# Cross attention: memory keys projected among the output projection, queries in a row, memory values behind them, head norms taken from raw projections

## The chip, the cores and the metric

The kernel runs on one core of a Trainium2 chip. What is measured is the device time of one execution in microseconds (us). Before the change it is 1073.2 us, the median of three runs (1072.76 to 1074.09).

The engines are named as in the profile: PE is TensorE's matmul side and PEld its weight loads, DVE is VectorE, ACT is ScalarE, POOL is GpSimd, and SP issues the DMAs. Each engine works through its own queue in the order in which the program put its instructions there, and waits on semaphores for the others.

## The reference, cut to what matters

One layer: three token mixers and a gated sum of them, an output projection with a residual, cross attention into a memory of 256 tokens, and a gated MLP. x has 512 tokens of 1024 channels. The change lies in the stretch from the output projection to the first matmuls of the MLP.

```python
def rmsnorm(x, g):
    xf = x.astype(jnp.float32)
    y = xf * lax.rsqrt(jnp.mean(xf * xf, axis=-1, keepdims=True) + EPS)
    return (y * g.astype(jnp.float32)).astype(x.dtype)

def memory_cross_attention(h, m, w_q, w_kv, q_g, k_g, w_o):
    q = rmsnorm(heads(h @ w_q, MEM_HEADS), q_g)          # 4 heads of 128
    k, v = jnp.split(m @ w_kv, 2, axis=-1)
    k = rmsnorm(heads(k, MEM_HEADS), k_g)
    v = heads(v, MEM_HEADS)
    s = jnp.einsum("bqhd,bkhd->bhqk", q, k).astype(jnp.float32) * MEM_DIM ** -0.5
    p = jax.nn.softmax(s, axis=-1).astype(v.dtype)
    o = jnp.einsum("bhqk,bkhd->bqhd", p, v).reshape(B, S, MEM_W)
    return o @ w_o

x = x + mixed @ w_out[l]
x = x + memory_cross_attention(rmsnorm(x, norm_xq[l]), rmsnorm(mem, norm_mem[l]), ...)
x = x + conv_ffn(rmsnorm(x, norm_ffn[l]), ...)
```

A norm over a row multiplies it by one number. The query of a head is the projection of a normed row, normed again over the head's 128 channels, so the first norm's factor cancels out of the second except in its epsilon.

## The kernel before

**Layout.** Channels lie on the 128 partitions and tokens along the free axis, so a projection of 1024 channels to 128 is eight blocks of 128x128 weights against tiles of 512 tokens (256 for the memory). A unit is 128x1024 weights, 512 KB, loaded into `wraw` (three buffers). Every matmul of a projection is done in float32r with both operands split into a high and a low part: `split_unit` makes `whi` on ACT (line 154) and `wlo` on DVE (line 155), two buffers each; activations are split by `split` and `split_scaled`. `mm3` then issues, for each block, whi times the high part (line 175) and whi times the low part (line 176), and at the end wlo times the high parts (line 178): 24 matmuls for each unit.

**The stages around the change.** `wo0` to `wo7` are the eight tiles of the output projection. After each, `residual` adds x on DVE (line 770), squares on ACT (line 772), and splits the result for the next projection (`xqh` on ACT, line 167; `xql` on DVE, line 168). The memory is loaded at this point too (`mem_sb`), split into `memh`/`meml` and squared. The norms' sums over channels are matmuls with a matrix of ones in plain float32: `memps` (line 783), `xqps` (line 799), `xfps` (line 871), and, inside each head, `mkn0p` to `mkn3p` and `mqn0p` to `mqn3p` (line 229, the `light` form of `head_norm`). `rsqrt` makes the factor with Ln, Exp and Square on ACT (lines 216 to 218) and two instructions on DVE (219, 220).

**The heads.** The string `CROSS` gives the order in which the steps are written: k is a key head (`memory_key`: projection `mk`, times `r_mem` on DVE, head norm), q a query head (`memory_query`: projection `mq`, times `r_xq` on DVE, head norm), w the weights of a head (`memory_weights`), v the values (`memory_values`: `mv`, four units of weights for two tiles of 128 tokens). `memory_weights` treats a head in two halves g: scores `msc` in float32 (line 829), row maxima on DVE (830), Exp on ACT (833, each followed by a read of the accumulated sum), reciprocal and scaling on DVE (834, 836), four transposes `mT` on PE (840) and a copy `mpt` on ACT (842). Then `mo` (line 860) multiplies with the values, `ym` splits the result, and `wmo0` to `wmo7` project back. `up` is the MLP's first projection; its outputs are multiplied with `r_f`, the factor from `xfps`, on DVE (line 885).

**What sets the order.** The code's order is not the order of the queues: a scheduler moves instructions on each engine after its own estimate of when they can run. PSUM is shared out in pools: three banks for projections (`d`), three for sums and scores (`m`), two for the transposes (`g`); a tile waits for the reader of the one whose bank it takes. In the row names a trailing number is a head or a unit, then a half: `msc21` is head 2, second half; `whi97` is the high part of unit 97, the first of `wmo`.

Of the kernel before, what the change touches and what calls it, by code (L numbers as in the profile page):

```python
# [9 lines left out]
F32 = mybir.dt.float32  # L10
# [12 lines left out]
CROSS = "k0 q0 k1 q1 w0 k2 q2 w1 k3 q3 w2 w3 v"  # L23
# [43 lines left out]
def build(nc, tc, ctx, x_t, mem_t, w, cols_d, const_d, unit_d, out_t, dbg=None):  # L67
# [14 lines left out]
    work = tiles_of("work", "n", 4)        # short-lived  # L82
# [30 lines left out]
    def in_one_go(after, tiles, func):  # L113
        """func on tiles in place, behind the instruction `after`, with one load of its table"""
        with tc.issue_after(after.ins), tc.high_priority():
            for t in tiles:
                S.activation(t, t, func)
            exp_ln_tables()
# [11 lines left out]
    eps = col("eps")  # L130
    gains = cols[:, COLS["fox_q"]:COLS["onorm"] + 1]
# [5 lines left out]
    units = {}  # L137

# [9 lines left out]
    def split_unit(u):  # L148
        """a unit of the weight stream as an exact sum of two float32r operands"""
        raw = units.pop(u) if u in units else load_unit(u)  # L150
        hi = wp.tile([P, 1024], F32R, tag="whi", name=f"whi{u}", bufs=WB[1])
        lo = wp.tile([P, 1024], F32R, tag="wlo", name=f"wlo{u}", bufs=WB[2])
        for s in [slice(0, T), slice(T, 2 * T)] if u == 0 else [slice(0, 2 * T)]:
            S.activation(hi[:, s], raw[:, s], AF.Copy)  # L154
            V.tensor_tensor(lo[:, s], raw[:, s], hi[:, s].bitcast(F32), ALU.subtract)  # L155
        return hi, lo

    def split(src, alloc, name):
        """src as hi + lo"""
        hi = alloc(name + "h", F32R)  # L160
        lo = alloc(name + "l", F32R)
        S.activation(hi, src, AF.Copy)
        V.tensor_tensor(lo, src, hi.bitcast(F32), ALU.subtract)
        return hi, lo
# [6 lines left out]
    def mm3(ps, unit, blocks, xs, first, last):  # L171
        """ps += the blocks of a unit times xs, without the product of the low parts"""
        hi, lo = unit
        for i, (b, (xh, xl)) in enumerate(zip(blocks, xs)):
            PE.matmul(ps, hi[:, b], xh, start=first and i == 0, stop=False)  # L175
            PE.matmul(ps, hi[:, b], xl, start=False, stop=False)  # L176
        for i, (b, (xh, _)) in enumerate(zip(blocks, xs)):
            PE.matmul(ps, lo[:, b], xh, start=False, stop=last and i == len(xs) - 1)  # L178
# [24 lines left out]
    def project_heads(u, ys, name, n=4):  # L203
        """[512, 1024] weights, two output tiles in a unit"""
        for g in range(n):
            unit = split_unit(u + g)
            for q in range(2):
                ps = dense_ps(f"{name}{2 * g + q}")
                mm3(ps, unit, [block(4 * q + k) for k in range(4)], ys, True, True)
                yield 2 * g + q, ps  # L210

    def rsqrt(ps, name, scale, n=T, work=work):
        """-2 / sqrt(ps * scale + eps), with a Newton step"""
        a = work(name + "a", F32, n)
        b = work(name + "b", F32, n)
        S.activation(a, ps, AF.Ln, bias=eps, scale=scale)
        S.activation(a, a, AF.Exp, scale=-0.5)
        S.activation(b, a, AF.Square, scale=math.sqrt(scale))
        V.scalar_tensor_tensor(b, ps, EPS / scale, b, ALU.add, ALU.mult)
        V.scalar_tensor_tensor(a, b, -3.0, a, ALU.add, ALU.mult)  # L220
        return a

    def head_norm(src, name, scale, n=T, work=work, psum=misc_ps, light=False):
        """-2 / sqrt(sum of src^2 * scale + eps) on every partition"""
        sq = work(name + "s", F32, n)
        S.activation(sq, src, AF.Square)
        ps = psum(name + "p")
        if light:
            PE.matmul(ps[:, :n], ones, sq, start=True, stop=True)
        else:  # L230
            hi, lo = split(sq, lambda name, dt: work(name, dt, n), name)
            PE.matmul(ps[:, :n], ones_r, hi, start=True, stop=False)
            PE.matmul(ps[:, :n], ones_r, lo, start=False, stop=True)
        return rsqrt(ps[:, :n], name, scale, n, work)
# [107 lines left out]
    def convolve(g, base):  # L342
        """silu(conv(projection)) of the tiles of q, k or v"""
        conv[g] = cs = [ptile(f"{g}{h}") for h in range(H)]
        for h in range(H):
            t, c, w = raws[g][h], conv[g][h], 4 * (base + h)
            last = S.activation(c, t, AF.Copy, scale=col("gdn_conv", w + 3))
            for i in (1, 2, 3):
                V.scalar_tensor_tensor(c[:, i:], t[:, :T - i], col("gdn_conv", w + 3 - i), c[:, i:], ALU.mult, ALU.add)
        in_one_go(last, cs, AF.Silu)  # L350

# [9 lines left out]
    def scalars():  # L361
# [25 lines left out]
        # token on partition: [.., token block, row]  # L387
# [5 lines left out]
        # beta, beta * exp(gc), exp(g_last - gc)  # L393
# [4 lines left out]
    def select(ps, kind, h, stop=True):  # L398
        """a row of the scalars on every partition"""
# [20 lines left out]
    def prep_head(h):  # L420
# [6 lines left out]
        # the decay, [j, i] by chunks, 0 for j > i  # L427
# [13 lines left out]
        # A^T without its factors beta_i, and attn^T  # L441
# [15 lines left out]
        # token-major keys and values  # L457
# [13 lines left out]
    # the inverses of the 32 x 32 diagonal blocks of I + A by elimination, a block's  # L471
    # even or odd columns on a partition
# [30 lines left out]
    def expand(dst, src, h):  # L503
        """the 32 x 32 blocks of a head on the diagonals of its chunks"""
# [13 lines left out]
    def invert(h):  # L518
        """(I + A)^-T of the chunks from that of the blocks on their diagonals: with D these and
        M = A D^-1 without these blocks, M^4 = 0 and (I + A)^-1 = D^-1 (I - M + M^2 - M^3)"""  # L520
# [47 lines left out]
    def qkv_head(u, h, name, norm, alloc):  # L568
        """q^T, k^T and [key, dv] by key blocks"""
# [20 lines left out]
    def packed(name, kinds):  # L590
        """[P, 128], .. [P, 512] of each kind, the halves of a kind's tile shared"""
# [191 lines left out]
    PE.matmul(ps[:, :M], ones, acc, start=True, stop=True)  # L783
    for t in range(2):
        PE.matmul(ps[:, M + t:M + t + 1], acc[:, t * P:t * P + P], ones[:, 0:1], start=True, stop=True)
    r_mem = ztile("r_mem")
    V.tensor_scalar(r_mem[:, :M + 2], rsqrt(ps[:, :M + 2], "rmem", 1.0 / D, M + 2), -0.5, None, ALU.mult)

# [1 line left out]
    acc = None  # L790
    xq = []
    for m in range(KC):
# [3 lines left out]
        xq.append(s)  # L796
    x2 = xr
    ps = misc_ps("xqps")
    PE.matmul(ps, ones, acc, start=True, stop=True)
    r_xq = cp.tile([P, T], F32, tag="rh", name="r_xq")  # L800
    V.tensor_scalar(r_xq, rsqrt(ps, "rxq", 1.0 / D), -0.5, None, ALU.mult)

# [1 line left out]
    def memory_key(h):  # L804
        ps = project(UNITS["mk"] + h, xs_mem, f"mk{h}", M)
        if h % 2 == 0:
            mem_k.append(ztile(f"memk{h}"))
        kn = mem_k[h // 2][:, h % 2 * M:h % 2 * M + M]
        V.tensor_tensor(kn, ps[:, :M], r_mem[:, :M], ALU.mult)
        r = head_norm(kn, f"mkn{h}", 1.0 / P, M, work=nwork, light=True)  # L810
        V.scalar_tensor_tensor(kn, kn, col("mk"), r, ALU.mult, ALU.mult)

    def memory_query(h):
        ps = project(UNITS["mq"] + h, xq, f"mq{h}")
        q = ztile(f"mqT{h}")
        V.tensor_tensor(q, ps, r_xq, ALU.mult)
        r = head_norm(q, f"mqn{h}", 1.0 / P, work=nwork, light=True)
# [28 lines left out]
    def memory_values():  # L846
        for t, ps in enumerate(project_tokens(UNITS["mv"], xs_mem, "mv", 2)):
            v = vwork(f"memv{t}")
            S.activation(v, ps, AF.Copy, scale=r_mem[:, M + t:M + t + 1])
            mem_v.append(v)  # L850

    mem_k, mem_v, qs, pts = [], [], [], []
    for step in CROSS.split():
        {"k": memory_key, "q": memory_query, "w": memory_weights, "v": lambda h: memory_values()}[step[0]](int(step[1:] or 0))
# [16 lines left out]
    PE.matmul(ps, ones, acc, start=True, stop=True)  # L871
# [55 lines left out]
def unit_columns():  # L927
    """[P, 32, 16]: the even (on even partitions) or odd columns of the unit matrix"""
# [4 lines left out]
def layout(inputs):  # L933
# [3 lines left out]
    def tiles(a, n):  # L937
        """[K, M] -> [units, P, 1024] streaming (output tile, k chunk) blocks of [P, 128]"""
# [88 lines left out]
```

## Time and profile before

| | |
|---|---|
| median of three runs | 1073.2 us |
| profiled execution: span from first to last instruction | 1072.4 us |
| PE busy | 1055.4 us, 98% of the span |
| DVE, ACT busy | 638.3 us, 556.3 us |
| output projection, wo0 to wo7 | 556.62 to 602.11 |
| keys, queries, values, weights of head 0 and scores of head 1 | 602.11 to 656.07 |
| from the last value matmul to the first wmo matmul | 656.07 to 676.18 |
| wmo0 to wmo7 | 676.18 to 699.54 |
| MLP | 699.54 to the end |

Times in a stage are from the start of the span. A row of the timeline gives the start, the length, the engine, the line, the operation and the tiles (out<-in); "x8" are eight instructions in a row, and then the length goes to the end of the last. PE starts a matmul before the one before it has ended, so what a matmul costs is the distance between starts, not its length. "[2.47 <-DVE mp L836]" is idle time of the engine ahead of the row, and what ended it. In a table of stretches each engine has its busy time and, in brackets, the count of instructions; PEclk is the granted TensorE clock as a share of 2.4 GHz.

### The profile page before, as it was taken

To read this page: it belongs to the slowest core of one execution; us is meant where nothing else is said; L and a number is where in the kernel's file an instruction comes from. 1 tells how busy PE (TensorE), PEld (TensorE's weight loads), DVE (VectorE), ACT (ScalarE), POOL (GpSimd) and SP (SyncE) were. 2 spreads that over 40 slices of the span, in tenths; PEclk is the share of its full clock that TensorE was granted. 3 is DMA by queue.
4 is the path that set the end of the run, shared out by engine and by line. 5 is a ranking of instruction groups with operands and counts; after the bars stand their busy time and mean duration, and the time that the engine had idled before them with its cause. 6 is when DMAs were issued, how large, how long until landed. Compare 5 with 4: busy or idle time off the path is not lost.

```text
span 1072.4 us, 12705 instructions
## 1 busy us (share of the span) xinstructions
PE 1055.4 (98%) x4868; PEld 858.3 (80%) x4868; DVE 638.3 (60%) x1002; ACT 556.3 (52%) x894; POOL 31.6 (3%) x81
## 2 busy tenths in 40 slices
PE   6999999999999999999999998999999999999998
PEld 4887888778888888888888886778888888888886
DVE  5987566886454443454577667667776667742221
ACT  6689677856263646574546557544444444431110
POOL 0000100101010000000000000000000000000000
PEclk9999999999999999999999999999999999999999
DMA  5232212121211122122244233122222222233330
GB/s 209 79 98 98 79 61 77 61 88 59 80 59 60 59 64 74 60 65 97 94 147 168 90 107 99 41 97 99 90 90 95 98 99 92 91 103 108 118 117 20
DMA packets 27853, 96.33 MB, mean 90 GB/s; under 512 B 3088, under 2 KB 3344, under 8 KB 27536
## 3 DMA queue, kind: packets, MB, share of 16 engines
q1 hardware_dynamic: 27648, 95.26, 27.1%
q8 instruction: 38, 0.62, 0.2%
q10 hardware_dynamic: 144, 0.26, 0.1%
q14 instruction: 23, 0.19, 0.1%
HBM read 93.41 MB, written 2.10 MB: 89 GB/s over the span
## 4 chain that ended last, share of the span: by engine, by line
PE 96%; DVE 1%; ACT 1%; DMA 1%; issue 0%; SPq 0%; DVEq 0%; ACTq 0%
PE up L176 8%; PE up L178 8%; PE up L175 8%; PE g L176 4%; PE g L175 4%; PE g L178 4%; PE dn L178 4%; PE dn L176 4%; PE dn L175 4%; PE wo L176 1%; PE s L175 1%; PE f L178 1%; PE f L175 1%; PE s L176 1%; PE wo L178 1%; PE wo L175 1%
## 5 line engine op out<-in xcount | busy, mean ns | idle before, releaser
L154 ACT ACTIVATE whi<-wraw 128x1024 fp32r<-128x1024 f32 (+1 forms) x168 | 177.1, 1054 | 286.0 <-PE up L176 86.1
L155 DVE TENSOR_TENSOR wlo<-wraw,whi 128x1024 fp32r<-128x1024 f32 (+1 forms) x168 | 204.7, 1219 | 144.2 <-PE dn L178 49.2
L176 PE MATMUL up<-xfl,whi 128*128 128x512 f32 x352 | 139.3, 396 | 0.0
L175 PE MATMUL up<-xfh,whi 128*128 128x512 f32 x352 | 138.7, 394 | 0.0
L178 PE MATMUL up<-xfh,wlo 128*128 128x512 f32 x352 | 88.9, 395 | 0.0
L178 PEld LDWEIGHTS up<-xfh,wlo 128*128 128x128 f32 x352 | 66.3, 188 | 15.7 <-issue 0.2
L176 PEld LDWEIGHTS up<-xfl,whi 128*128 128x128 f32 x352 | 66.3, 188 | 15.7 <-issue 0.2
L175 PEld LDWEIGHTS up<-xfh,whi 128*128 128x128 f32 x352 | 66.3, 188 | 15.5
L175 PE MATMUL g<-hh,whi 128*128 128x512 f32 x192 | 76.9, 401 | 0.0
L176 PE MATMUL g<-hl,whi 128*128 128x512 f32 x192 | 76.8, 400 | 0.0
L889 DVE SCALAR_TENSOR_TENSOR uc<-u,cols,uc 128x511 f32<-128x511 f32 (+1 forms) x88 | 65.3, 747 | 1.4
L887 ACT ACTIVATE uc<-u,cols 128x512 f32<-128x512 f32 x44 | 35.8, 816 | 45.2 <-DVE u L885 45.0
L885 DVE TENSOR_TENSOR u<-up,r_f 128x512 f32<-128x512 f32 x44 | 30.2, 688 | 40.4 <-PE up L178 40.4
L178 PE MATMUL g<-hh,wlo 128*128 128x512 f32 x192 | 52.3, 402 | 0.0
L178 PEld LDWEIGHTS g<-hh,wlo 128*128 128x128 f32 x192 | 35.9, 188 | 8.3 <-issue 0.2
L176 PEld LDWEIGHTS g<-hl,whi 128*128 128x128 f32 x192 | 36.2, 188 | 7.8 <-issue 0.2
L175 PEld LDWEIGHTS g<-hh,whi 128*128 128x128 f32 x192 | 36.2, 188 | 7.7
L175 PE MATMUL f<-hh,whi 128*128 128x512 f32 x64 | 26.0, 406 | 0.0
L175 PE MATMUL s<-hh,whi 128*128 128x512 f32 x64 | 25.7, 402 | 0.0
L176 PE MATMUL s<-hl,whi 128*128 128x512 f32 x64 | 25.5, 398 | 0.0
L176 PE MATMUL wo<-msl,whi 128*128 128x512 f32 x64 | 25.3, 396 | 0.0
L176 PE MATMUL f<-hl,whi 128*128 128x512 f32 x64 | 25.3, 395 | 0.0
(968 smaller groups left out, 2288.1 us busy)
## 6 DMA issues: line engine op xcount, KB each, us to landing
wraw<-w SPq DMA_DIRECT2D x166, 512.0 KB, 3.3
x<-x_t SPq DMA_DIRECT2D x8, 256.0 KB, 7.2
xr<-x_t SPq DMA_DIRECT2D x2, 1024.0 KB, 6.2
out<-out SPq DMA_DIRECT2D x8, 256.0 KB, 2.0
mem_sb<-mem_t SPq DMA_DIRECT2D x4, 256.0 KB, 6.5
wraw<-w SPq DMA_DIRECT2D x2, 256.0 KB, 4.7
inv<-unit ACTq DMA_DIRECT2D x1, 256.0 KB, 3.9
const<-const SPq DMA_DIRECT2D x1, 194.0 KB, 6.4
```

The costliest lines, as they stand in the source:

```text
L154: S.activation(hi[:, s], raw[:, s], AF.Copy)
L155: V.tensor_tensor(lo[:, s], raw[:, s], hi[:, s].bitcast(F32), ALU.subtract)
L175: PE.matmul(ps, hi[:, b], xh, start=first and i == 0, stop=False)
L176: PE.matmul(ps, hi[:, b], xl, start=False, stop=False)
L178: PE.matmul(ps, lo[:, b], xh, start=False, stop=last and i == len(xs) - 1)
L885: V.tensor_tensor(u, ps, r_f, ALU.mult)
L887: S.activation(c, u, AF.Identity, bias=col("ffn_conv_b", j), scale=col("ffn_conv", 3 * j + 2))
L889: V.scalar_tensor_tensor(c[:, s:], u[:, :T - s], col("ffn_conv", 3 * j + 2 - s), c[:, s:], ALU.mult, ALU.add)
```

## The change

- `CROSS` loses its keys: they are written after output tiles 2, 3, 4 and 5 (`KEYS_AFTER`), each as projection, norm and gain. Then come the four queries, the weights of heads 0 and 1, the values, and the weights of heads 2 and 3.
- Keys and queries are no longer multiplied with `r_mem` and `r_xq`. ACT copies the raw projection out of PSUM, and `raw_norm` takes the head's mean square of the raw values plus an epsilon that carries the first norm's mean square (`e_mem`, `e_xq`, one ACT instruction each).
- The sums over channels `memps`, `xqps`, `xfps` and those of the heads are made in float32r from a split of the squares, two matmuls in place of one float32 matmul, with one more ACT and one more DVE instruction each (`column_sums`, `raw_norm`).
- The value projections are held behind the last matmul of the last query (`issue_after`).
- POOL sets one more constant (`eps2`) at the start.

```diff
-CROSS = "k0 q0 k1 q1 w0 k2 q2 w1 k3 q3 w2 w3 v"
+KEYS_AFTER = (2, 3, 4, 5)
+CROSS = "q0 q1 q2 q3 w0 w1 v w2 w3"
...
+    def column_sums(ps, src, name, n=T, work=work):
+        hi, lo = split(src, lambda name, dt: work(name, dt, n), name)
+        PE.matmul(ps, ones_r, hi, start=True, stop=False)
+        PE.matmul(ps, ones_r, lo, start=False, stop=True)
...
-    PE.matmul(ps[:, :M], ones, acc, start=True, stop=True)
+    column_sums(ps[:, :M], acc, "memacc", M)
...
-    r_mem = ztile("r_mem")
-    V.tensor_scalar(r_mem[:, :M + 2], rsqrt(ps[:, :M + 2], "rmem", 1.0 / D, M + 2), -0.5, None, ALU.mult)
+    e_mem = ztile("e_mem")
+    S.activation(e_mem[:, :M], ps[:, :M], AF.Identity, bias=eps2, scale=EPS / D)
+    r_mem = cp.tile([P, 2], F32, tag="r_mem", name="r_mem")
+    V.tensor_scalar(r_mem, rsqrt(ps[:, M:M + 2], "rmem", 1.0 / D, 2), -0.5, None, ALU.mult)
+    def raw_norm(src, name, e, n):
+        sq = nwork(name + "s", F32, n)
+        S.activation(sq, src, AF.Square)
+        hi, lo = split(sq, lambda name, dt: nwork(name, dt, n), name)
+        ps = misc_ps(name + "p")[:, :n]
+        PE.matmul(ps, ones_r, hi, start=True, stop=False)
+        PE.matmul(ps, ones_r, lo, start=False, stop=True)
+        a, b = awork(name + "a", F32, n), awork(name + "b", F32, n)
+        V.scalar_tensor_tensor(sq, ps, 1.0 / P, e, ALU.mult, ALU.add)
+        S.activation(a, sq, AF.Ln)
+        S.activation(a, a, AF.Exp, scale=-0.5)
+        S.activation(b, a, AF.Square)
+        V.tensor_tensor(b, sq, b, ALU.mult)
+        V.scalar_tensor_tensor(a, b, -3.0, a, ALU.add, ALU.mult)
+        return a
+    def memory_key(h):
+        ps = project(UNITS["mk"] + h, xs_mem, f"mk{h}", M)
...
+        S.activation(kn, ps[:, :M], AF.Copy)
+        r = raw_norm(kn, f"mkn{h}", e_mem[:, :M], M)
+        V.scalar_tensor_tensor(kn, kn, col("mk"), r, ALU.mult, ALU.mult)
...
     for m in range(KC):
         ps = project(UNITS["wout"] + m, ms, f"wo{m}")
...
+        if m in KEYS_AFTER:
+            memory_key(KEYS_AFTER.index(m))
...
-        V.tensor_tensor(q, ps, r_xq, ALU.mult)
-        r = head_norm(q, f"mqn{h}", 1.0 / P, work=nwork, light=True)
+        S.activation(q, ps, AF.Copy)
+        r = raw_norm(q, f"mqn{h}", e_xq, T)
...
-        for t, ps in enumerate(project_tokens(UNITS["mv"], xs_mem, "mv", 2)):
+        with tc.issue_after(last_mm[0]):
+            psv = project_tokens(UNITS["mv"], xs_mem, "mv", 2)
+        for t, ps in enumerate(psv):
...
-    PE.matmul(ps, ones, acc, start=True, stop=True)
+    column_sums(ps, acc, "xf")
```

The built programs are the same on every engine up to the output projection, but for the constant on POOL, and again from the MLP's second pair of projections on. In between the queues differ at many places; two of them follow. The line numbers of the changed program are four to thirty higher for the same code.

On PE, in the output projection, before: the end of the high-part matmuls of `wo2`, and `wo3` behind it.

```order
L176 MATMUL wo2_4844<-msl4_4680,whi79_4847 128x512
L175 MATMUL wo3_4881<-msh0_4669,whi80_4884 128x512
L176 MATMUL wo3_4881<-msl0_4670,whi80_4884 128x512
L175 MATMUL wo3_4881<-msh0_4669,whi80_4884 128x512
L178 MATMUL wo2_4844<-msh0_4669,wlo79_4848 128x512 x4
L178 MATMUL wo2_4844<-msh4_4679,wlo79_4848 128x512 x4
```

The same place now (`mk0` is the first key's projection; its operands `memh` and `meml` are the split memory):

```order
L180 MATMUL wo2_4853<-msl4_4682,whi79_4856 128x512
L179 MATMUL mk0_4890<-memh0_4711,whi89_4893 128x256
L182 MATMUL wo2_4853<-msh0_4671,wlo79_4857 128x512 x4
L182 MATMUL wo2_4853<-msh4_4681,wlo79_4857 128x512 x4
L180 MATMUL mk0_4890<-meml0_4712,whi89_4893 128x256
```

The first key's first matmul now stands where the third tile of the output projection gave way to the fourth, ahead of the third tile's low-part matmuls, and the rest of the key is spread around `wo3`.

On ACT, around the last value weights, before (`mqn2` is the norm of query head 2, `mp10` and `mp11` are the Exps of head 1, `memv` the copies of the values):

```order
L154 ACTIVATE whi96_5647<-wraw96_5645 128x1024
L842 ACTIVATE mpt00_5275<-mT00_5270 128x512
L842 ACTIVATE mpt01_5294<-mT01_5289 128x512
L216 ACTIVATE mqn2a_5378<-mqn2p_5376,cols_73 128x512
L217 ACTIVATE mqn2a_5378<-mqn2a_5378 128x512
L218 ACTIVATE mqn2b_5379<-mqn2a_5378 128x512
L833 ACTIVATE mp10_5387,mm10_5388<-msc10_5386,mm10_5388 128x256 x2
L154 ACTIVATE whi97_5705<-wraw97_5703 128x1024
L833 ACTIVATE mp11_5406,mm11_5407<-msc11_5405,mm11_5407 128x256 x2
L226 ACTIVATE mkn3s_5456<-memk2_5327 128x256
L849 ACTIVATE memv0_5663<-mv0_5589,r_mem_4760 128x512
L849 ACTIVATE memv1_5665<-mv1_5590,r_mem_4760 128x512
```

The same place now (`mp00` and `mp01` are the Exps of head 0):

```order
L158 ACTIVATE whi96_5626<-wraw96_5624 128x1024
L158 ACTIVATE whi97_5760<-wraw97_5758 128x1024
L808 ACTIVATE mqn3a_5483<-mqn3s_5474 128x512
L861 ACTIVATE mp00_5493,mm00_5494<-msc00_5492,mm00_5494 128x256 x2
L861 ACTIVATE mp01_5512,mm01_5513<-msc01_5511,mm01_5513 128x256 x2
L879 ACTIVATE memv0_5642<-mv0_5568,r_mem_4769 128x512
L809 ACTIVATE mqn3a_5483<-mqn3a_5483 128x512
L879 ACTIVATE memv1_5644<-mv1_5569,r_mem_4769 128x512
L158 ACTIVATE whi98_5805<-wraw98_5803 128x1024
L810 ACTIVATE mqn3b_5484<-mqn3a_5483 128x512
L861 ACTIVATE mp10_5531,mm10_5532<-msc10_5530,mm10_5532 128x256 x2
```

Before, head 0's Exps had been made well ahead of this place, its transposes' copies stood behind the last value weights, and head 1's Exps stood on both sides of `whi97`, the first weights of the projection back, ahead of the copies of the values. Now `whi97` stands ahead of head 0's Exps, and head 1's Exps stand behind the values' copies and `whi98`.

## Rows read from the trace of the kernel before

**Rows 1.** Page, busy time, share of the span and instructions of PE.

```profile
PE 1055.4 (98%) x4868; PEld 858.3 (80%) x4868; DVE 638.3 (60%) x1002; ACT 556.3 (52%) x894; POOL 31.6 (3%) x81
```

**Rows 2.** Table of stretches: bounds, length, busy time of each engine (instructions), clock, DMA.

```profile
core 0: us, PE busy (x) PEld busy (x) DVE busy (x) ACT busy (x) POOL busy (x), PEclk, DMA share, GB/s
556.62:602.11 45.49, 45.49 (x199) 37.00 (x198) 31.21 (x50) 24.81 (x43) 0.00 (x0) 1.00 0.47 162
602.11:656.07 53.96, 53.96 (x280) 44.92 (x278) 34.15 (x60) 31.02 (x57) 0.00 (x0) 1.00 0.34 108
656.07:676.18 20.11, 16.47 (x74) 12.18 (x72) 14.23 (x35) 14.61 (x38) 0.00 (x0) 0.92 0.16 53
```

**Rows 3.** Waits of PE from 600 on: total, times, longest.

```profile
PE mT L840 <- DVE mp L836: 2.5, 1, 2.5
```

**Rows 4.** Timeline of PE behind the values: start, length, engine, instruction.

```profile
659.23 0.60 PE L840 MATMUL mT<-const,mp 128*128 128x128 f32 x4
659.66 1.03 PE L860 MATMUL mo<-mpt,memv 128*128 128x256 f32 x4
...
662.73 1.89 PE L829 MATMUL msc<-memk,mqT 128*128 128x256 f32 x8
667.08 0.63 PE L840 MATMUL mT<-const,mp 128*128 128x128 f32 x4 [2.47 <-DVE mp L836]
668.01 3.50 PE L829 MATMUL msc<-memk,mqT 128*128 128x256 f32 x8 [0.30 <-DVE mm L834]
```

**Rows 5.** Table of stretches, two microseconds each, behind the longest wait.

```profile
668.00:670.00 2.00, 1.99 (x5) 1.65 (x6) 0.59 (x2) 0.34 (x1) 0.00 (x0) 0.50 0.00 0
...
672.00:674.00 2.00, 1.43 (x10) 0.91 (x8) 1.34 (x7) 1.57 (x8) 0.00 (x0) 1.00 0.00 0
```

**Rows 6.** Timeline of PE: matmuls in float32r, and sums and scores in float32.

```profile
600.25 2.02 PE L178 MATMUL wo<-msh,wlo 128*128 128x512 f32 x8
602.11 0.28 PE L175 MATMUL mk<-memh,whi 128*128 128x256 f32 x1
...
604.01 1.11 PE L178 MATMUL mk<-memh,wlo 128*128 128x256 f32 x8
604.95 0.40 PE L175 MATMUL mq<-xqh,whi 128*128 128x512 f32 x1
...
637.04 1.02 PE L229 MATMUL mqn1p<-mqn1s,ones 128*128 128x512 f32 x2
637.90 1.89 PE L829 MATMUL msc<-memk,mqT 128*128 128x256 f32 x8
639.44 1.74 PE L178 MATMUL mq<-xqh,wlo 128*128 128x512 f32 x6
```

**Rows 7.** Timeline of ACT among the values: norm, Exps, weights, copies.

```profile
652.25 0.63 ACT L217 ACTIVATE mqn2a<-mqn2a 128x512 f32<-128x512 f32 x1
...
653.45 0.46 ACT L833 ACTIVATE mp<-msc,mm 128x256 f32<-128x256 f32 x1
...
654.35 1.06 ACT L154 ACTIVATE whi<-wraw 128x1024 fp32r<-128x1024 f32 x1
655.29 0.47 ACT L833 ACTIVATE mp<-msc,mm 128x256 f32<-128x256 f32 x1
...
656.50 1.27 ACT L849 ACTIVATE memv<-mv,r_mem 128x512 f32<-128x512 f32 x2
```

**Rows 8.** Timeline of DVE behind the values: a row maximum, a pair of scalings.

```profile
664.66 0.69 DVE L830 TENSOR_REDUCE mm<-msc 128x2 f32<-128x512 f32 x1
...
666.59 0.61 DVE L836 TENSOR_SCALAR mp<-mp,mm 128x256 f32<-128x256 f32 x2
```

**Rows 9.** Timelines of DVE and of PE at the start of the MLP.

```profile
714.42 1.29 DVE L885 TENSOR_TENSOR u<-up,r_f 128x512 f32<-128x512 f32 x2
...
717.12 0.40 PE L175 MATMUL up<-xfh,whi 128*128 128x512 f32 x1
```

**Rows 10.** Timeline of DVE: the last piece of the memory's split.

```profile
576.71 0.48 DVE L168 SCALAR_TENSOR_TENSOR meml<-mem_sb,cols,memh 128x256 fp32r<-128x256 f32 x1
```

More of the change, by code (lines that the diff above doesn't have):

```diff
@@ L130, in build @@
     eps = col("eps")
+    eps2 = cp.tile([P, 1], F32, tag="eps2", name="eps2")
+    G.memset(eps2, EPS * EPS)
     gains = cols[:, COLS["fox_q"]:COLS["onorm"] + 1]
@@ L137, in build @@
     units = {}
+    last_mm = []
     def load_unit(u):
@@ L177, in mm3 @@
         for i, (b, (xh, _)) in enumerate(zip(blocks, xs)):
-            PE.matmul(ps, lo[:, b], xh, start=False, stop=last and i == len(xs) - 1)
+            mm = PE.matmul(ps, lo[:, b], xh, start=False, stop=last and i == len(xs) - 1)
+        last_mm[:] = [mm.ins]
     def block(i, n=P):
@@ L221, in rsqrt, with head_norm @@
         return a
-    def head_norm(src, name, scale, n=T, work=work, psum=misc_ps, light=False):
+    def column_sums(ps, src, name, n=T, work=work):
+        hi, lo = split(src, lambda name, dt: work(name, dt, n), name)
+        PE.matmul(ps, ones_r, hi, start=True, stop=False)
+        PE.matmul(ps, ones_r, lo, start=False, stop=True)
+    def head_norm(src, name, scale, n=T, work=work, psum=misc_ps):
         sq = work(name + "s", F32, n)
@@ L227, in head_norm @@
         ps = psum(name + "p")
[L228 to L233, printed above, removed]
+        column_sums(ps[:, :n], sq, name, n, work)
         return rsqrt(ps[:, :n], name, scale, n, work)
@@ L782, in build @@
     ps = misc_ps("memps")
-    PE.matmul(ps[:, :M], ones, acc, start=True, stop=True)
+    column_sums(ps[:, :M], acc, "memacc", M)
     for t in range(2):
         PE.matmul(ps[:, M + t:M + t + 1], acc[:, t * P:t * P + P], ones[:, 0:1], start=True, stop=True)
-    r_mem = ztile("r_mem")
-    V.tensor_scalar(r_mem[:, :M + 2], rsqrt(ps[:, :M + 2], "rmem", 1.0 / D, M + 2), -0.5, None, ALU.mult)
+    e_mem = ztile("e_mem")
[19 more added lines that the diff above has]
+        ps = project(UNITS["mk"] + h, xs_mem, f"mk{h}", M)
+        if h % 2 == 0:
+            mem_k.append(ztile(f"memk{h}"))
+        kn = mem_k[h // 2][:, h % 2 * M:h % 2 * M + M]
+        S.activation(kn, ps[:, :M], AF.Copy)
+        r = raw_norm(kn, f"mkn{h}", e_mem[:, :M], M)
+        V.scalar_tensor_tensor(kn, kn, col("mk"), r, ALU.mult, ALU.mult)
     acc = None
-    xq = []
+    xq, mem_k = [], []
     for m in range(KC):
@@ L796, in build @@
         xq.append(s)
+        if m in KEYS_AFTER:
+            memory_key(KEYS_AFTER.index(m))
     x2 = xr
     ps = misc_ps("xqps")
-    PE.matmul(ps, ones, acc, start=True, stop=True)
[L800 to L811, printed above, removed]
+    column_sums(ps, acc, "xq")
+    e_xq = cp.tile([P, T], F32, tag="rh", name="e_xq")
+    S.activation(e_xq, ps, AF.Identity, bias=eps2, scale=EPS / D)
     def memory_query(h):
@@ L846, in memory_values @@
     def memory_values():
-        for t, ps in enumerate(project_tokens(UNITS["mv"], xs_mem, "mv", 2)):
+        with tc.issue_after(last_mm[0]):
+            psv = project_tokens(UNITS["mv"], xs_mem, "mv", 2)
+        for t, ps in enumerate(psv):
             v = vwork(f"memv{t}")
-            S.activation(v, ps, AF.Copy, scale=r_mem[:, M + t:M + t + 1])
+            S.activation(v, ps, AF.Copy, scale=r_mem[:, t:t + 1])
             mem_v.append(v)
-    mem_k, mem_v, qs, pts = [], [], [], []
+    mem_v, qs, pts = [], [], []
     for step in CROSS.split():
-        {"k": memory_key, "q": memory_query, "w": memory_weights, "v": lambda h: memory_values()}[step[0]](int(step[1:] or 0))
+        {"q": memory_query, "w": memory_weights, "v": lambda h: memory_values()}[step[0]](int(step[1:] or 0))
     ym = []
@@ L870, in build @@
     ps = misc_ps("xfps")
-    PE.matmul(ps, ones, acc, start=True, stop=True)
+    column_sums(ps, acc, "xf")
     r_f = cp.tile([P, T], F32, tag="rl", name="r_f")
```

## The prediction

> **What bounds the kernel now.** I read the page's busy times first: PE works 98% of the span [rows 1], so only matmuls taken away, or PE idle time, can pay. The table of stretches says where each is to be had [rows 2]. In the output projection (556.62 to 602.11) and from there to the last value matmul (656.07) PE is busy for the whole length. In the 20.11 us behind the values it works 16.47 and is idle for 3.6. The list of PE's waits has one large entry there, 2.47 us in which PE waits for DVE's scaling of the Exps [rows 3]; the timeline gives its place, ahead of transposes, and 0.30 more right behind it [rows 4]. Behind the large one the granted clock stands at 0.50 [rows 5], which is the lower level, 1.2 GHz, and the score matmuls that follow take 3.50 us where they took 1.89 before [rows 4]: 1.6 us more.
>
> **Prices of matmuls, as distances between starts.** Eight float32r matmuls of 512 columns take 1.86 us, 0.232 each; eight of 256 columns 0.94, 0.118 each; one plain float32 sum of 512 columns takes 637.90 - 637.04 = 0.86; eight float32 score instructions (two halves of a head, 256 columns) take 1.54, so 0.77 a half and 0.385 for a sum of 256 columns, which is two instructions [rows 6]. The four transposes of a half take 0.43 [rows 4]; the values' products are as wide as the scores, 0.77 a half.
>
> **The sums over channels.** A float32 sum becomes two float32r matmuls: 0.86 - 0.464 = 0.40 saved at 512 columns (four queries, `xqps`, `xfps`: 2.4 us), 0.385 - 0.236 = 0.15 at 256 (four keys, `memps`: 0.75 us), 3.15 us in all, and as PE is never idle in the first two stages what lies there comes off the end one for one. The Trainium skill, "FP8 and Floating Point Precision", section "TensorE Precision Notes", says that true float32 makes four passes; by that a sum of 512 columns would cost 4 x 0.232 = 0.93, the saving would be 0.46 and 0.24, and 3.96 us in all. The rows show 3.7 passes at 512 columns and 3.3 at 256, so I keep 3.15.
>
> The splits add one ACT and one DVE instruction for each sum, and the raw copy moves one instruction a head from DVE to ACT. At 0.63 us on ACT [rows 7] and 0.69 on DVE [rows 8] this lies under PE. With the four keys the output projection's stage grows to some 57 us, in which DVE has 31.2 + 11.6 = 43 us and ACT 24.8 + 13 = 38 us to do, the first terms from the table [rows 2], the second estimated from the instructions moved in.
>
> **The keys in the output projection.** Their matmuls are neither fewer nor shorter; they are only moved, at no price as long as PE finds operands. By the new order `mk0` begins behind two wo tiles of 24 x 0.232 = 5.57 and the 16 high-part matmuls of `wo2`, 3.7: 14.9 after 556.62, so at 571.5 or a little later. Its first half stands ahead of `wo3` and its second half behind `wo3`'s high-part matmuls. The last piece of the memory's split was done at 576.71 + 0.48 = 577.2 before [rows 10]; the matmuls that want it stand behind all of `wo2`, half of `mk0` and 24 of `wo3`, 571.5 + 1.9 + 1 + 5.6 = 580. What is moved past: SP issues the four key units between the wo units, one key unit ahead of the next wo unit, with three `wraw` buffers; ACT and DVE split them between the residuals. A late `whi` would cost about its own length, 0.95 us (two starts of 655.29 - 654.35 on ACT [rows 7]). I find each whi and wlo done before PE comes to it and take 0; bounds 0 and 4 us (all four keys late).
>
> **Up to the end of the values.** PE is gapless there before, and the queries in a row leave it work (the next query, then the values) through every norm's chain. So the end moves by work alone. Two score halves are now behind the values: -1.54. Two transposed halves: -0.86. `xqps` -0.40, `memps` -0.15. Of the keys' sums three of 0.385 become four of 0.236: -0.21. Of the queries' three of 0.86 become four of 0.464: -0.72. Sum -3.88, so PE is done with the values at T = 652.2 where it was 656.07.
>
> **Behind the values**, what is left is heads: six score halves, eight transposed halves, seven halves of products ahead of `wmo0`: 6 x 0.77 + 8 x 0.43 + 7 x 0.77 = 13.45 us of PE work. I followed the new queues one against the other:
> - On ACT, `whi97` stands ahead of head 0's Exps (order rows above). It takes the buffer of the third value unit, so it can't start until that unit's matmuls are through, at T - 2.6; then 0.94, a Ln, four Exps with their reads of 0.45, a copy of the values 0.57, an Exp, the second copy, `whi98` 0.94, a Square, and head 1's Exps of 0.9: these end at T + 5.0, by the lengths in [rows 7].
> - PE in that time has head 1's and half of head 2's scores and head 0's transposes. The next scores, `msc21`, need the bank of `msc10`, the third in use, which head 1's first Exps free. PE is out of work at T + 3.15 and waits 1.95.
> - `msc30` then waits for the last query's gain on DVE, about 0.5.
> - The transposes of head 2 wait for a PSUM bank behind a copy on ACT that itself stands behind an Exp waiting for a row maximum on DVE (0.69 a maximum, 0.52 a scaling, by their starts [rows 8]): about 1.6.
>
> Waits: 4.05. 13.45 + 4.05 = 17.5. The same sum over the tail of before is 12.3 of work (four score halves, six transposed, seven products, two sums), 3.6 idle and 1.6 of slow clock = 17.5, against the true 20.11: 2.6 us are lost in pieces that I can't place. Between 0 and 2.6 I take 1.1, since part of them are starts behind waits, which the new tail has too. That gives 18.6, `wmo0` at 652.2 + 18.6 = 670.8, and -5.4.
>
> **The projection back and the MLP.** `xfps` saves 0.40. Its factor reaches PE only through the banks of the MLP's first tiles: before, DVE was through with `u` near 715.1 and PE took the next bank at 717.12 [rows 9], 2 us of slack, against some 1.3 us of one more ACT and DVE instruction. So it hides. Without that cover it would cost 1.3 less the slack that is left.
>
> Sum: -5.4 - 0.4 = -5.8; the span goes from 1072.4 to 1066.6. The median of the runs stands 0.8 above the profiled span, so 1067.4, and I say 1067.5. Upwards: the whole 2.6 in the tail and a slow-clock stretch of 1.6 leave -2.7, 1070.5. Downwards: no lost pieces (-1.1) and only the one wait of 1.95 (-2.1) give -9.0 at the most, 1064.2.
>
> **The rivals.**
> 1. *The clock falls once more behind the new wait.* Before, one wait of 2.47 us was followed by clock 0.50 and a price of 1.6 [rows 4, 5]; now PE waits 1.95 us. For it: the waits follow each other closely. Against: each is shorter. Time: 1067.5 + 1.6 = 1069.1. The Trainium skill, "TensorE: Matmul & The Clock Gate", section "Why this matters for your kernels", asks to avoid idle gaps between bursts of matmuls for this reason; the trace agrees, with its 0.50 behind 2.47 us.
> 2. *The keys starve PE in the output projection*, so that the change doesn't do there what it says. The memory's split ends at 577.2 [rows 10], and 12 units must be split where 8 were. At 0.95 us of a late `whi` a key, 3.8 us: 1071.3, within 0.2% of before. Against: a DVE load of 43 in 57 us.
> 3. *Slower: the tail stays at 1.2 GHz.* With three waits in a row where there was one large one, the clock falls at the first and does not come back before `wmo0`. Of 13.45 us of work some 10.9 lie behind the first wait; at half clock they take 10.9 more, of which 1.9 cover waits: +9.0, 1076.5. It decides once more than 7.7 us of matmuls run at half clock (5.8 + 1.9). Against: before, the clock was back at 1.00 four us after it fell, with 0.57 us of PE idle in the two us in which it was back [rows 5], and stood at 0.92 over the stage as a whole [rows 2].
> 4. *A larger gain*: the small waits don't show, and the lost pieces were all due to the large wait: the lower bound above, 1064.2 to 1066.
>
> **How the numbers follow.** Forecast (1066 to 1069) 0.60, rival 1 0.20, rival 2 0.09, rival 3 0.06, rival 4 0.05. The range holds the forecast and rival 1 with their bounds and most of rival 4, and stops short of rivals 2 and 3: 1064.7 to 1071.0. About 0.2%, 2.1 us, is what a measurement of this kernel can tell from no change. Faster by more than that (below 1071.1): the forecast, rival 1 and rival 4, less a share of 0.03 for their upper ends, 0.82. Within 0.2%: rival 2 and that share, 0.12. Slower: rival 3, 0.06.
>
> **What would show it.** In the profile of after: PE without idle time from 556 to the last value matmul, in the keys among the output projection above all (step: keys moved at no price); the matmul behind the values starting near 652.2; sums of two float32r matmuls at 0.46 and 0.24; the first wait behind the values near 2 us with ACT's Exp as its releaser, and smaller ones with DVE and ACT; the granted clock at 1.00 around them; `wmo0` at 670.8; MLP stage the same but for 0.4. The prediction is wrong if PE idles among the `wo` tiles, or if the table shows the lower clock over several microseconds behind the values.

## The result

| | before | after |
|---|---|---|
| median of the runs timed together | 1073.38 us (4 runs) | 1067.57 us (4 runs, 1065.86 to 1068.22) |
| ratio | | 0.9943, 95% interval 0.9929 to 0.9957 |
| profiled execution: span | 1072.4 us | 1064.1 us |
| PE busy | 1055.4 us | 1049.7 us |
| wait entries of PE from the output projection on | 2.47, 0.63, 0.30, 0.21 us | 1.27, 0.56 us |

The median fell by 5.8 us, and 1067.5 was forecast. The profiled executions lie further apart, by 8.2 us (the runs of 1074.09 and 1065.86). Both are right, and the section on the prediction takes the difference apart.

The page of after, its first line on PE, which answers to [rows 1]:

```profile
PE 1049.7 (99%) x4868; PEld 857.2 (81%) x4868; DVE 641.6 (60%) x1010; ACT 561.7 (53%) x912; POOL 31.6 (3%) x82
```

The table of stretches of after, from the first output tile to the end of the values, from there to `wmo0`, to the MLP, and to the end. Columns as in [rows 2]:

```profile
555.88:651.23 95.35, 95.35 (x466) 79.63 (x465) 67.90 (x109) 59.80 (x111) 0.00 (x0) 1.00 0.41 138
651.23:668.36 17.13, 15.27 (x86) 12.93 (x84) 14.15 (x43) 15.04 (x44) 0.00 (x0) 1.00 0.19 62
668.36:691.71 23.35, 23.35 (x103) 19.00 (x101) 16.05 (x23) 11.45 (x18) 0.00 (x0) 1.00 0.21 68
691.71:1064.10 372.39, 368.72 (x1587) 298.60 (x1585) 207.11 (x258) 132.95 (x162) 0.00 (x0) 1.00 0.28 94
```

The first stretch has no idle PE, though four keys are in it: 95.35 us where [rows 2] adds up to 45.49 + 53.96 = 99.45. The tail behind the values is 17.13 where it was 20.11, and its granted clock is 1.00 where it was 0.92. Behind it `wmo` is as long as before, 23.35 us for 23.36, and the MLP is 0.4 us shorter.

PE behind the values in after (timeline; the release in brackets), answering to [rows 4]:

```profile
651.23 1.89 PE L857 MATMUL msc<-memk,mqT 128*128 128x256 f32 x8
652.95 0.38 PE L868 MATMUL mT<-const,mp 128*128 128x128 f32 x2
653.17 1.03 PE L857 MATMUL msc<-memk,mqT 128*128 128x256 f32 x4
654.04 0.82 PE L868 MATMUL mT<-const,mp 128*128 128x128 f32 x6
656.13 1.13 PE L857 MATMUL msc<-memk,mqT 128*128 128x256 f32 x4 [1.27 <-ACT mp L861]
...
663.72 0.66 PE L868 MATMUL mT<-const,mp 128*128 128x128 f32 x4 [0.56 <-ACT mpt L870]
```

The 1.27 us stand where the 1.95 were forecast, ahead of `msc21`, and an Exp of ACT ends them, as forecast. On ACT the queue reads as the order did:

```profile
648.63 1.06 ACT L158 ACTIVATE whi<-wraw 128x1024 fp32r<-128x1024 f32 x1 [3.93 <-PE mv L205]
649.59 0.62 ACT L808 ACTIVATE mqn3a<-mqn3s 128x512 f32<-128x512 f32 x1
650.11 0.46 ACT L861 ACTIVATE mp<-msc,mm 128x256 f32<-128x256 f32 x1
...
655.49 0.50 ACT L861 ACTIVATE mp<-msc,mm 128x256 f32<-128x256 f32 x1
```

`whi97` waits for the third value unit's matmuls until 648.63 = T - 2.6 (T is 651.23 here), head 0's Exps stand behind it, and head 1's first pair ends at 655.99, T + 4.8.

### The profile page after: what moved, and what is told of

Its sections match the earlier page's. It is cut to its first block, busy times and chain, and to the rows that moved or that the text cites. A ratio compares the mean times of both kernels' runs of the same rounds, so it can differ in the third digit from the quotient of the medians.

```text
span 1064.1 us, 12730 instructions
## 1 busy us (share of the span) xinstructions
PE 1049.7 (99%) x4868; PEld 857.2 (81%) x4868; DVE 641.6 (60%) x1010; ACT 561.7 (53%) x912; POOL 31.6 (3%) x82
## 4 chain that ended last, share of the span: by engine, by line
PE 97%; DVE 1%; DMA 1%; ACT 0%; SPq 0%; issue 0%; ACTq 0%
PE up L179 8%; PE up L182 8%; PE up L180 8%; PE g L180 4%; PE g L179 4%; PE g L182 4%; PE dn L182 4%; PE dn L179 4%; PE dn L180 4%; PE f L182 1%; PE f L179 1%; PE s L179 1%; PE wo L182 1%; PE wo L180 1%; PE s L180 1%; PE wo L179 1%
```

## The experiments

All times are medians. "The stretch" is the distance from the first matmul of `wo0` to the first of the MLP in the profiled execution: 142.92 us before, 135.83 after. It leaves out the MLP and the start of the program: in the four profiles of the changed kernel `wo0` starts between 555.31 and 556.17.

**The changed kernel again, three more profiles** (no edit).

> The changed kernel once more, for its spread and a second profile. If the 2.4 us between its executions come from the tail behind the values (the clock falling once behind the first wait in some executions, 1.6 us), a second profile may show 0.50 or 0.72 there and wmo0 1.6 us later against the last value matmul. If they come from ahead of the change, the tail is 17.1 us again and the start of the output projection moves. Median 1067.6 either way.

> The changed kernel for a third profile. Its first two profiled executions (1065.9 and 1066.2) agree within 0.02 us in every stretch from the output projection to the start of the MLP, and the unprofiled ones lie up to 2.4 us higher. If a profile falls on one of those, the time is in the MLP: matmuls at 0.2333 us in place of 0.2324, as in the profiles of late_whi97 and keys_late, 1.5 us over 372; the stretch of the change is the same 135.8. If it's the tail's clock, the stretch is 137.4.

> The changed kernel for a fourth profile. Three profiled executions lay at 1065.3 to 1066.2, all with 0.2324 us a matmul in the MLP; its unprofiled ones go up to 1068.2. If this one lies above 1067, its MLP shows 0.2333 and takes 374 us; if it is at 1066 again, 372.4 and 0.2324.

Measured: 1067.22 (five runs, 1065.86 to 1068.04; ratio 0.9943, 0.993 to 0.9957), 1065.29 and 1065.71. All four profiles agree in the stretch within 0.01 us (135.83, 135.83, 135.83, 135.82) and in the MLP within 0.05. This is the fourth:

```profile
555.74:651.08 95.34, 95.34 (x465) 79.62 (x464) 67.91 (x109) 59.80 (x111) 0.00 (x0) 1.00 0.41 138
651.08:668.21 17.13, 15.27 (x86) 12.92 (x84) 14.15 (x43) 15.04 (x44) 0.00 (x0) 1.00 0.19 62
...
691.56:1064.00 372.44, 368.72 (x1587) 298.60 (x1585) 207.14 (x258) 132.93 (x162) 0.00 (x0) 1.00 0.28 94
```

The four profiled executions lie at 1065.3 to 1066.2. Of the seven others one is at 1065.86 and six are at 1067.2 to 1068.2, and no profile fell on one of these. What they do otherwise is not shown. It isn't the slower clock: the mean granted clock of all eleven is 1.000 or 0.999, while 33 of the 54 runs of before that were timed beside the experiments show 0.998. Three other kernels below show what it may be.

**Plain sums in the changed kernel.** In both places the split and the two matmuls become one matmul:

```diff
-        hi, lo = split(sq, lambda name, dt: nwork(name, dt, n), name)
-        PE.matmul(ps, ones_r, hi, start=True, stop=False)
-        PE.matmul(ps, ones_r, lo, start=False, stop=True)
+        PE.matmul(ps, ones, sq, start=True, stop=True)
```

> The changed kernel with its eleven sums over channels made again by one plain float32 matmul each (the splits of the squares gone, all else kept). If the sums lie on PE's path as counted, 6 x 0.40 + 5 x 0.15 = 3.15 us come back: 1070.7. By four passes for float32 it would be 3.96: 1071.5. If the sums are hidden, or if the splits' longer chains cost as much as the matmuls save, nothing: 1067.6.

Measured: 1068.01, ratio 0.9949 (0.9937 to 0.9962), between the two expectations. The profile tells why (stretches as above, to `wmo0`):

```profile
556.27:656.06 99.79, 99.79 (x474) 81.98 (x472) 66.56 (x107) 58.36 (x107) 0.00 (x0) 1.00 0.38 132
656.06:670.12 14.06, 13.16 (x78) 11.32 (x76) 10.99 (x35) 12.73 (x37) 0.00 (x0) 1.00 0.22 76
```

The stretch is 137.20, 1.37 longer. PE works 136.30 in it in place of 133.97, 2.33 more where the prices give 2.75, and idles 0.90 in place of 1.86, 0.96 less. So the matmuls are there, but the longer chains of the split sums had been paid for in the tail. With 0.4 more in the MLP the two profiles are 1.8 us apart from `wo0` on. The medians are only 0.8 apart, and in the changed kernel's the runs of 1067.2 to 1068.2 count, which no profile shows.

**The keys behind the output projection:**

```diff
-KEYS_AFTER = (2, 3, 4, 5)
-CROSS = "q0 q1 q2 q3 w0 w1 v w2 w3"
+KEYS_AFTER = ()
+CROSS = "k0 k1 k2 k3 q0 q1 q2 q3 w0 w1 v w2 w3"
```

> The changed kernel with the four keys written behind the output projection, one after the other, ahead of the queries. If moving the keys only moves PE work between two stretches without gaps, it costs nothing: 1067.6, within 0.5. If the place of the keys is what brought the rest of the gain beyond the sums, 2.65 us come back: 1070.2.

Measured: 1066.0, ratio 0.9931 (0.9919 to 0.9943): not dearer but 1.2 us under the changed kernel's 1067.22 of the same chip, with intervals that overlap. In the stretch the two profiles are 1.51 us apart (134.32 against 135.83).

```profile
556.49:652.54 96.05, 96.05 (x470) 80.61 (x468) 69.71 (x113) 63.47 (x117) 0.00 (x0) 1.00 0.38 137
652.54:667.37 14.83, 14.36 (x81) 11.90 (x80) 12.07 (x38) 12.86 (x37) 0.00 (x0) 1.00 0.21 72
667.37:690.81 23.44, 23.44 (x102) 18.96 (x101) 16.33 (x23) 11.39 (x18) 0.00 (x0) 1.00 0.19 68
690.81:1064.80 373.99, 370.24 (x1587) 297.72 (x1585) 207.31 (x258) 132.99 (x162) 0.00 (x0) 1.00 0.26 93
```

PE works as long in the stretch (133.85 against 133.97) and idles 0.47 in place of 1.86. So the keys' place costs PE no work, and the gain is idle time in the tail, where the scheduler set head 1's first scores ahead of the last value unit. The last two rows show the other thing: `wmo` takes 23.44 and the MLP 373.99 with the same matmuls, the clock at 1.00 and no wait. That is 0.4% for each matmul, 0.2333 us in place of 0.2324.

**Unit 97 later on ACT.** Its load stays; its split is held behind head 1's Exps:

```diff
+    units[UNITS["mo"]] = load_unit(UNITS["mo"])
+    with tc.issue_after(last_exp[1]):
+        first = split_unit(UNITS["mo"])
```

> The changed kernel with the high part of unit 97 held behind head 1's Exps on ACT instead of ahead of head 0's. If that instruction is what the first wait behind the values (1.27 us) is made of, the wait falls by its 0.95 to 0.3: 1066.6. If DVE, which is busy all the time from 655 to 663, is the next bound there, PE waits as long a little later: 1067.5.

Measured: 1065.15, ratio 0.9926 (0.9914 to 0.9939), under both expectations. PE's waits in it:

```profile
PE msc L857 <- ACT whi L158: 0.7, 1, 0.7
...
PE mo L891 <- ACT mpt L871: 0.3, 1, 0.3
PE msc L857 <- ACT mp L861: 0.2, 1, 0.2
```

The wait for head 1's Exps falls from 1.27 to 0.24 as expected, but other entries of 0.72 and 0.30 come up behind it, so the tail only falls from 17.13 to 16.57. The one of 0.72 ends, by the profile, with unit 97's own instruction, which now runs from 655.87 to 656.94 on ACT: most of the wait has moved with it. So the wait was made of this instruction, as the first reading had it, and its new place costs as well. The rest of the 2.1 us between the medians (1067.22 and 1065.15) isn't in the stretch. Its profiled execution is its slowest, 1066.95, with the MLP at 373.91; the other four lie at 1065.0 to 1065.2.

**The old order, with all of the new arithmetic.** `KEYS_AFTER` empty, the values not held back, and

```diff
-CROSS = "q0 q1 q2 q3 w0 w1 v w2 w3"
+CROSS = "k0 q0 k1 q1 w0 k2 q2 w1 k3 q3 w2 w3 v"
```

> The changed kernel with keys, queries, weights and values written in the order of before (keys among the queries, values last), the norms from raw projections and the split sums kept. If the sums' 3.15 us are all that the arithmetic brings and the new order brings the other 2.65, this is 1073.4 - 3.15 = 1070.2, and up to 1071.2 if the splits' longer chain to the last query shows in the tail. If the order is worth nothing: 1067.5.

Measured: 1073.36, ratio 1.0002 (0.9993 to 1.0011): nothing, against 1070.2 expected.

```profile
555.66:653.18 97.52, 97.52 (x481) 81.85 (x480) 68.65 (x118) 63.49 (x121) 0.00 (x0) 1.00 0.39 135
653.18:674.28 21.10, 14.87 (x69) 11.91 (x68) 13.62 (x33) 13.05 (x34) 0.00 (x0) 0.92 0.14 50
674.28:698.85 24.57, 23.88 (x103) 18.87 (x101) 15.63 (x22) 11.34 (x18) 0.00 (x0) 1.00 0.19 65
```

Its list of PE's waits:

```profile
PE mT L868 <- DVE mp L864: 5.9, 4, 2.8
PE wmo L179 <- ACT ym3h L166: 0.7, 1, 0.7
PE mo L889 <- ACT mpt L870: 0.4, 1, 0.4
```

PE is done with the values 1.9 us sooner than in [rows 2], and gives it back: the tail is 21.10, with 5.9 us of waits for DVE's scaling of the Exps and the clock at 0.92, and `wmo` waits 0.7 for the last head.

**The split sums alone, in the kernel before** (norms and order as they were):

```diff
-            PE.matmul(ps[:, :n], ones, sq, start=True, stop=True)
+            hi, lo = split(sq, lambda name, dt: work(name, dt, n), name)
+            PE.matmul(ps[:, :n], ones_r, hi, start=True, stop=False)
+            PE.matmul(ps[:, :n], ones_r, lo, start=False, stop=True)
```

> The kernel before with only the eleven sums made in float32r from split squares; norms, order and values as before. 3.15 us of PE work less: 1070.2. The last query's norm has one ACT and one DVE instruction more (1.3 us) ahead of the scores on which the tail waits: 1071.5. If the sums are hidden altogether: 1073.4.

Measured: 1082.62, ratio 1.0081 (1.0067 to 1.0095), 9 us slower, which no theory had. PE's waits, the tail as a whole, and two pieces of it:

```profile
PE mkn3p L235 <- ACT mkn3h L162: 4.7, 1, 4.7
PE msc L836 <- DVE mqT L825: 4.3, 1, 4.3
PE mqn2p L235 <- ACT mqn2h L162: 1.3, 1, 1.3
...
648.81:682.25 33.44, 22.04 (x94) 17.71 (x92) 21.50 (x52) 22.50 (x57) 0.00 (x0) 0.85 0.09 32
...
663.00:665.00 2.00, 2.00 (x9) 1.80 (x8) 0.00 (x0) 1.93 (x5) 0.00 (x0) 0.50 0.04 8
673.00:679.00 6.00, 5.74 (x18) 4.69 (x19) 3.70 (x13) 2.08 (x8) 0.00 (x0) 0.50 0.00 0
```

Three of the four heads' scores now come behind the values, and there the chains of the last two heads are bare; that the scheduler moved them because it reckons with the longer chains is my reading. PE waits for the split of a square (4.7) and for the last query (4.3), and behind each of the two the granted clock stands at 0.50, 1.2 GHz. The profiled execution is the fastest of the four; the others took 1082.15 to 1083.32.

**The order alone, in the kernel before:**

```diff
-CROSS = "k0 q0 k1 q1 w0 k2 q2 w1 k3 q3 w2 w3 v"
+CROSS = "k0 k1 k2 k3 q0 q1 q2 q3 w0 w1 v w2 w3"
```

> The kernel before with only the order of the heads changed: four keys, four queries, the weights of heads 0 and 1, values, weights of heads 2 and 3; norms and float32 sums as before. The run of old_order gave nothing for the arithmetic without the order (143.2 us from the first output tile to the MLP against 142.9). If the order alone brings the rest, this stretch is 137 to 138 as in f32_sums, and the time 1068 to 1069. If the order pays only with raw norms, since otherwise the first norm's factor holds up all four queries and every score comes to stand behind the values, there are 15 us of head work there in place of 13.45 and about 2 us of waits: stretch 139.7, 1070. If neither does it alone: 1073.3.

Measured: 1071.31, ratio 0.9982 (0.9973 to 0.9991), 2.0 us faster.

```profile
PE msc L829 <- DVE mqn3b L219: 1.8, 1, 1.8
PE mqn3p L229 <- ACT mqn3s L226: 0.6, 1, 0.6
...
651.92:672.44 20.52, 18.35 (x94) 14.59 (x95) 17.41 (x50) 16.41 (x48) 0.00 (x0) 1.00 0.12 42
```

The stretch is 140.37. All eight halves of scores stand behind the values, as expected where the first norm's factor holds up the queries. In the run with plain sums, which has norms from raw projections, it is 137.20; but there the keys stand in the output projection and the values are held back too.

**Head 0's weights ahead of the last query, late keys** (expected to be faster):

```diff
-CROSS = "k0 k1 k2 k3 q0 q1 q2 q3 w0 w1 v w2 w3"
+CROSS = "k0 k1 k2 k3 q0 q1 q2 w0 q3 w1 v w2 w3"
```

> The kernel with late keys, and head 0's weights written ahead of the last query, so that head 0's scores, Exps and transposes and head 1's scores stand among the value matmuls. Behind the values there are 4 score halves, 5 transposed halves and 7 of products: 10.6 us in place of 13.45 behind the values of the changed kernel. If PE is then without work no longer than now (1.9 us), about 1.5 us less than the changed kernel or 0.5 less than the late keys: 1065.3. If the last query's chain sets the end of the tail whatever stands ahead of it, PE waits the 2.8 us that it has lost in work: 1067.5.

Measured: 1071.72, ratio 0.9981 (0.9973 to 0.999), over 4 us slower than the changed kernel, a miss on both sides.

```profile
PE mT L868 <- ACT mpt L870: 1.9, 1, 1.9
PE mo L890 <- ACT mpt L870: 1.4, 2, 0.7
PE mT L868 <- DVE mp L864: 1.1, 1, 1.1
...
654.50:670.30 15.80, 12.18 (x65) 10.02 (x64) 12.53 (x32) 11.99 (x32) 0.00 (x0) 1.00 0.09 34
670.30:696.26 25.96, 24.59 (x106) 19.24 (x105) 15.63 (x22) 11.85 (x18) 0.00 (x0) 1.00 0.18 61
```

There is less work behind the values (12.18 us), but PE idles 3.6 in it, 1.4 more among `wmo` and 0.6 among the values: with less work to stand over them, the chains of the last two heads show.

**Late keys and late unit 97 together** (both edits).

> Late keys and unit 97's high part behind head 1's Exps together. Alone they gave 1066.0 and 1065.15. With late keys PE waits only 0.5 us behind the values, so if PE's work is the floor there is no more than that to get: stretch 133.9 after 134.3, and 1065.0 to 1066.0 by the MLP's two pitches. If the two add up (1.5 and 0.5 in the stretch): 133.8 and the same.

Measured: 1063.99 (1063.39 to 1064.39), ratio 0.9913 (0.9899 to 0.9926). This is the fastest kernel of the study, 9.3 us below before.

```profile
652.04:666.39 14.35, 14.00 (x81) 12.02 (x80) 12.37 (x36) 13.42 (x38) 0.00 (x0) 1.00 0.24 74
666.39:689.75 23.36, 23.36 (x103) 19.01 (x102) 16.05 (x23) 11.46 (x18) 0.00 (x0) 1.00 0.22 68
689.75:1062.20 372.45, 368.71 (x1587) 298.60 (x1585) 207.14 (x258) 132.92 (x162) 0.00 (x0) 1.00 0.28 94
```

The stretch is 133.76 with 0.35 us of idle PE left. The edits add up there (1.51 and 0.47 alone, 2.07 together).

**Plain sums in that fastest kernel** (both edits, and the one of the run with plain sums).

> Late keys and unit 97 behind head 1's Exps, with the eleven sums as one plain float32 matmul each. In the changed kernel plain sums cost 1.37 us of the stretch and not the 2.75 of PE work that were counted, since PE then waited 0.96 us less behind the values. Where PE waits only 0.35 us there is nothing of that kind to give back: 2.3 to 2.75 in the stretch, 136.1 to 136.5 after 133.76, 0.4 more in the MLP, 1066.7 to 1067.1. If the matmuls themselves are worth less than counted, the stretch is 135.1 as before and the time 1065.8.

Measured: 1068.48, ratio 0.9957 (0.9943 to 0.997), 4.5 us slower, more than either expectation.

```profile
PE mo L889 <- ACT mpt L869: 0.8, 2, 0.5
PE wmo L179 <- ACT ym3h L166: 0.7, 1, 0.7
...
638.03 1.02 PE L803 MATMUL mqn2p<-mqn2s,ones 128*128 128x512 f32 x2
638.49 1.26 PE L182 MATMUL mq<-xqh,wlo 128*128 128x512 f32 x3
639.59 0.39 PE L203 MATMUL mv<-whi,memh 128*128 128x512 f32 x1
```

A sum and three matmuls from 638.03 to 639.59 are 1.56 us; less 3 x 0.232 that is 0.86 for the sum, the price of [rows 6]. So the price holds. The stretch is 138.62, 4.86 longer: PE works 3.71 more, where the prices give 2.75, and idles 1.15 more, 0.46 of it in the tail and 0.69 among `wmo`, where the scheduler set the last head's products so late that PE waits for their split. With the price of 0.43 for a sum of 256 columns that the next section comes to, the prices give 3.0; the rest of the work, 0.7 us, I can't place.

## Why the prediction came out

**The keys in the output projection: right.** No idle PE among the `wo` tiles, and the keys behind the projection cost the same PE time (133.85 against 133.97). Rival 2 falls.

**Up to the end of the values: right.** -3.88 was forecast. From `wo0` to the end of the values after has 95.35 and before 99.45, so -4.10. Behind the difference is a price. The distance to the next start is not always what a matmul costs. A head's scores among the values, in the trace of before:

```profile
651.33 1.89 PE L829 MATMUL msc<-memk,mqT 128*128 128x256 f32 x8
652.87 0.58 PE L200 MATMUL mv<-whi,meml 128*128 128x512 f32 x1
653.28 0.62 PE L198 MATMUL mv<-whi,memh 128*128 128x512 f32 x2
```

The float32r matmul behind the eight starts after 1.54, and then the next start is 0.41 away in place of 0.23. Up to there, less one matmul of 0.23, the eight take 1.72. So a half costs 0.86 and not 0.77, and a sum of 256 columns 0.43 and not 0.385 (in the last kernel `mkn2p` and one matmul of the query take 615.23 to 615.89, less 0.23 again 0.43). A sum is so 3.6 times a float32r matmul of its width and not 3.3. With these prices the forecast would have been -4.24, 0.14 on the other side.

**The tail: right in its mechanism, wrong in two sizes that offset each other in part.** 18.6 was forecast and 17.13 measured. The two sizes are the waits, 4.05 by forecast and 1.83 in the trace, and the lost pieces, 1.1 and 1.85. The waits were 1.27 and 0.56 = 1.83 and not 4.05: PE had work until T + 3.6 and not T + 3.15, head 1's Exps came 0.2 sooner, the wait for the last query's gain didn't show as an entry, and the one for the transposes' bank was a third of what I had. The step that failed is the following of the queues, which came out too late at each of these. The lost pieces were 17.13 - 13.45 - 1.83 = 1.85 and not 1.1. Most of them have a place now, and it is the price of a half: eight score instructions take 651.23 to 652.95 = 1.72 and not 1.54, four 653.17 to 654.04 = 0.87 and not 0.77. Seven blocks of scores or products stand ahead of transposes in this tail, where the whole price shows from start to start, and they come to 1.1 us too much together; the rest lies around the two waits and at one change from transposes to scores.

**The clock (rivals 1 and 3).** The granted clock stayed at 1.00 through the tail in all four profiles, behind a wait of 1.27. The scores at the lower clock did take 1.6 us more in the trace of before, but of those 54 runs of before the 21 with a mean clock of 1.000 have a mean time of 1073.0 and the 33 with 0.998 one of 1073.6: 0.6 us apart, not 1.6. There is no profile of before without a fall, so where the other 1.0 goes isn't shown. Rival 3's mechanism exists in part: in the kernel with the sums alone the clock stands at 0.50 over six microseconds behind a wait of 4.3, but it is back at 1.00 before `wmo0`. The Trainium skill, "TensorE: Matmul & The Clock Gate", section "Why this matters for your kernels", warns of such gaps, and that trace agrees with it.

**The sum of the parts: the step that does not hold in general.** I wrote -3.15 for the sums and the rest for the tail, as if they could be added up. By the stretch:

| | order of before | keys, queries, values in a row |
|---|---|---|
| norms and sums of before | 142.92 | 140.37 |
| raw norms, plain sums | not run | 137.20 |
| raw norms, split sums | 143.19 | 135.83 |
| norms of before, split sums | 150.60 | not run |

(The keys stand behind the output projection in 140.37 and in it in 137.20 and 135.83, and the values are held back in 137.20 and 135.83 alone. By the run with late keys the keys' place costs PE no work, but it changes the waits by 1.4 us; the holding back of the values was not tried by itself.) With the order of before, the whole arithmetic loses 0.3, and the split sums alone lose 7.7. With the new order 3.2 us lie between the norms of before and the raw norms. How much of this is the norms' own is not shown: with late keys, unit 97 later, raw norms and plain sums the stretch is 138.62, only 1.75 under 140.37. The split sums bring 1.4 here and 0.4 in the MLP, and 4.9 between the last two kernels (138.62 and 133.76). In these kernels PE time saved in sums counts in full only where the tail behind the values doesn't wait for the chains that the saving lengthens.

**The end: 0.8 and 2.4.** I added the distance from the profiled span to the median of before, 0.8 us. That was the wrong bridge: each run is about 1.7 above its own span, so the profiled execution of before was the run of 1074.09, the slowest of the three shown, and the profiled one of after is the run of 1065.86, its fastest. Between these two the stretch gives -7.1, an earlier start -0.7 and the MLP -0.4, -8.2 in all, where I had -5.8. Between the medians it is -5.8, because six of the seven unprofiled runs of after lie at 1067.2 to 1068.2, above all profiled ones. That the median met the forecast to 0.1 us is partly luck: 1.5 us more in the tail were won than I had counted, and something as large is lost again in most runs. That it is the MLP's 0.2333 us a matmul, seen in the profiles of the late keys (373.99), of late unit 97 (373.91) and of the order alone, fits in size (1.5 us) and is not shown for this kernel.

## What to carry to other kernels

Where PE is the bound almost everywhere, look at the one stretch where it isn't, and ask of each saving which chain it lengthens there: the same eleven cheaper sums cost 9.3 us in one order of the work and gained 0.8 and 4.5 in two others. Here each head's chain through the softmax wanted long independent work to stand over it, and the last such chain was what had to start early. A table of stretches, with busy and idle PE side by side for each variant, showed that in one look; sums of saved instructions did not.

## What the runs showed of the hardware

- The same float32r matmuls, without a wait and at a granted clock of 1.00, ran at 0.2324 us in some profiled executions and 0.2333 in others, from `wmo` to the end (23.35 and 372.4 us, or 23.44 and 373.9). It changes within an execution too: by the starts from 612 to 630, all four profiles of the changed kernel ran at 0.2333 there and at 0.2324 in the MLP, and that of the late keys at 0.2325 there and at 0.2333 in the MLP. What sets it is open.
- Eight float32 matmul instructions of 256 columns cost 1.72 us and four 0.86. With transposes behind them that is the distance to the next start. With float32r matmuls behind them the next start comes after 1.54, and the 0.18 us that are missing show behind that start (0.41 for 0.23), with no entry among the waits.
- In the kernel before, runs with a mean granted clock of 0.998 were 0.6 us longer on average than those with 1.000, while the scores at the lower clock took 1.6 us more in the rows.
